# A hybrid decoder layer: mixer work placed as single hops between dense products, TensorE in program order

## The chip, the cores and the metric

The kernel runs on one core of a Trainium2 chip. Five engines work side by side, each through its own instruction queue: TensorE (matmuls, PE in the profile, its weight loads PEld), VectorE (DVE), ScalarE (ACT), GpSimd (POOL) and SyncE (SP), whose queue issues the DMA transfers here. The metric is the device time of one execution in microseconds, the median of several runs: 2523.2 us before (three runs, 2522.54 to 2525.14).

## The reference

One decoder layer over x of 2048 tokens by 1024 channels, all float32, conditioned by a vector c:

```python
mod = silu(c) @ w_ada + b_ada                       # six rows of 1024
shift1, scale1, gate1, shift2, scale2, gate2 = split(mod, 6)
h = rmsnorm(x, norm1_w) * (1 + scale1) + shift1
proj = h @ w_in          # 2312 columns: q 512, k 128, v 128, z 512, x/B/C 1024, dt 8
attn = sliding_window_attention(rope(q), rope(k), v, sinks)   # 8 query, 2 key heads, window 128
xbc = silu(causal_depthwise_conv(xbc, conv_w, conv_b))        # width 4
y = ssd_chunked_scan(xs, softplus(dt + dt_bias), -exp(a_log), B, C, d_skip)   # 8 heads, state 128, chunks of 128
y = groupnorm(y * silu(z)) * ssm_norm_w
x = x + gate1 * (concat(attn, y) @ w_out)
h = rmsnorm(x, norm2_w) * (1 + scale2) + shift2
x = x + gate2 * ((silu(h @ w_gate) * (h @ w_up)) @ w_down)    # 2816 hidden
return rmsnorm(x, final_norm_w)
```

The scan carries a state from chunk to chunk, so the SSD chunks depend on each other in order; attention looks at the chunk and the one before it.

## The kernel before

Tokens are cut into four blocks of 512 (b = 0 to 3), each of four tiles of 128. Every dense product is computed as three products: each float32 operand is split into a rounded part `hi` and the rest `lo` (`split`, `halves`, `weight`), and `mm3` (L216-219) accumulates hi x hi, hi x lo and lo x hi. `weight` (L203) loads 256 KB of a weight into `raw`, rounds it on ACT (L212) and subtracts on POOL (L213); each block does so again for all weights of the input and the output projection.

The **mixer phase** goes over the blocks. `in_proj(b, h)` yields after each dense piece: queries, keys and values (`tokens`, 256 or 264 columns a matmul), eight groups of convolution channels (L355, 24 matmuls of 512 columns each) and the gate z. Results go to DRAM. Beside it run the **mixers**, which are Python generators: `attentions(b)` (scores, softmax, values, on PSUM banks `at` and `am`) and `ssds(b)` (banks `st` and `sm`). A hop is a group of matmuls whose result an ACT or DVE instruction has to read before the next group can start. `beside` (L919) advances the mixers by `RATIO` = 1.6 steps per dense piece; one step holds several hops. `finish(ssd_of[b - 1])` (L953) runs what is left of a block's scan in blocks 1 and 2, before `out_proj(b - 1)`; the output projection of blocks 0 and 1 lies in this phase, that of blocks 2 and 3 in the down-projection. `ada` computes a row of `mod`: a 512 KB load and a product with the sum over the row, 16 rows ahead of the first block (eight of them shared between POOL and ACT), 32 later through the one buffer `aw`.

The **up-projection** (`quads`, `operands`, seven products in place of eight per 2 x 2 group, L753-755) runs for blocks 0 and 1, with the attention of block 3 and the scan of blocks 2 (its rest) and 3 beside it at `RATIO_UP` = 0.55 steps per product; then down-projections of blocks 0 and 1, the up-projection of blocks 2 and 3, and their down-projections.

What sets the order: the program is traced in Python order, and a planner then places the instructions of every engine, TensorE too, by a cost model and by when their inputs are due, so the order on an engine isn't that of the text. `issue_after` adds an edge on one engine. Within an engine the queue is strictly in order on the chip. Tile pools have a fixed number of buffers per tag (`w` 6, `raw` 5, `hl` 8, `it` 3, four PSUM banks `d`); a new tile waits until an old one's last reader is done.

Of the kernel before, what the change touches and what calls it, by code (L numbers as in the profile page):

```python
# [17 lines left out]
P = 128  # L18
# [13 lines left out]
RATIO, RATIO_UP = 1.6, 0.55  # L32
# [10 lines left out]
def hymba_layer(ctx, tc, xT, crow, pos, wada, vecs, rows, wq, wkv, wz, wx, wo, wgu, wd4, wd2, outT):  # L43
# [5 lines left out]
    sb = mixing.enter_context(tc.tile_pool(name="mix", bufs=1, side="right"))  # L49
    ip = projecting.enter_context(tc.tile_pool(name="inp", bufs=1))  # L50
# [22 lines left out]
    def m2(dt=F32):  # L73
        return big("m2", M2, dt)

    def m4():
        return sb.tile([P, 2, T], F32R, name="m4", tag="m4", bufs=M4)

    def m1():
        return small([P, 2 * P], "m1", M1)  # L80
# [30 lines left out]
    later_f = big("it", 3, pool=ip)[:, 0:P]  # L111
# [21 lines left out]
    for i in range(2):  # L133
        cs, th = csil[:, i * T:(i + 1) * T], big("it", 3, pool=ip)
        nc.scalar.activation(th, cs, AF.Tanh, scale=0.5)
        nc.vector.scalar_tensor_tensor(cs, th, 1.0, cs, ALU.add, ALU.mult)
    mod = const([P, 48], "mod", pool=cst)

    def ada(i, tag, bufs, shared=False):
        w = ip.tile([P, 2, T], F32, name=tag, tag=tag, bufs=bufs).rearrange("p h t -> p (h t)")  # L140
        load = nc.sync.dma_start(w, wada[i])
        m = mod[:, i:i + 1]
        if shared:
            nc.gpsimd.tensor_tensor(w, w, csil, ALU.mult)
            nc.scalar.activation(w, w, AF.Copy, scale=0.5, accum_out=m)
            nc.vector.tensor_tensor(m, m, b_ada[:, i:i + 1], ALU.add)
        else:
            nc.vector.tensor_tensor_reduce(w, w, csil, 0.5, b_ada[:, i:i + 1], ALU.mult, ALU.add, m)
        return load
# [10 lines left out]
    def rope_tables():  # L160
        posf = const([P, S // P], "posf", pool=ip)
        nc.vector.tensor_copy(posf, posi)
        ang = big("it", 3, pool=ip)
# [3 lines left out]
        for dst, turn in ((sin, 0.0), (cos, 0.25)):  # L167
            k, r = big("it", 3, pool=ip), big("it", 3, pool=ip)
# [34 lines left out]
    def weight(src, n=T, own=None):  # L203
        if own is None:
            raw = wt.tile([P, 528], F32, name="raw", tag="raw", bufs=RAW)
            two = wt.tile([P, 2, 528], F32R, name="w", tag="w", bufs=SPLIT)
        else:
            raw = own.tile([P, T], F32, name="rawo", tag="rawo", bufs=2)
            two = own.tile([P, 2, T], F32R, name="wo", tag="wo", bufs=2)
        hi, lo = two[:, 0, :n], two[:, 1, :n]  # L210
        nc.sync.dma_start(raw[:, :n], src)
        nc.scalar.activation(hi, raw[:, :n], AF.Copy)  # L212
        nc.gpsimd.tensor_tensor(lo, raw[:, :n], hi.bitcast(F32), ALU.subtract)  # L213
        return hi, lo
# [33 lines left out]
    def modulated(x, bc, scale, shift):  # L248
        h = tmp()
        nc.vector.scalar_tensor_tensor(h, x, scale, bc, ALU.mult, ALU.mult)  # L250
        hi, lo = pair("hl", 8, pool=ip)
# [8 lines left out]

    def norm1(b, h):
        acc = tmp()
        for d in range(KT):
            square_into(acc, load_x(b, d), d == 0)
        y = rstd(acc)
        yield
        bc = spread(y)
        for d in range(KT):
            h.append(modulated(load_x(b, d), bc, scl1[:, d:d + 1], sh1[:, d:d + 1]))
# [9 lines left out]
    def in_proj(b, h):  # L279
        dt_of[b] = small([P, NT, 8], "dt", 3)  # L280

        def tokens(srcs, n, toks):
            per = 2 if n == 256 else 1
            banks = [dense() for _ in range(len(toks) // per)]
            plan = [(i, t, banks[i // per][:, i % per * n:i % per * n + n]) for i, t in enumerate(toks)]
            for kp in range(KT // 2):
                whi, wlo = weight(srcs[kp], 2 * n)
                for e in range(2):
                    k, cs = 2 * kp + e, slice(e * n, (e + 1) * n)
                    for i, t, out in plan:  # L290
                        ts = slice(t * P, (t + 1) * P)
                        mm3(out, h[k][0][:, ts], h[k][1][:, ts], whi[:, cs], wlo[:, cs],
                            k == 0 and i % per == 0, k == KT - 1 and i % per == per - 1)
            return [(t, out) for _, t, out in plan]

        def tokens_by_k():
            qb = [dense() for _ in range(NT)]
            for kp in range(KT // 2):
                ws = [weight(wq[c][kp], 512) for c in range(2)]
# [8 lines left out]
            return qb  # L308

        def rope(dst, src, heads, gt):  # L310
            s4 = src.rearrange("p (h two j) -> p h two j", two=2, j=HALF)
            d4 = dst.rearrange("p (h two j) -> p h two j", two=2, j=HALF)
            tm = big("it", 3, pool=ip)[:, :heads * 64]
            t4 = tm.rearrange("p (h two j) -> p h two j", two=2, j=HALF)
            c = cos[:, gt, :].unsqueeze(1).broadcast_to([P, heads, HALF])
            s = sin[:, gt, :].unsqueeze(1).broadcast_to([P, heads, HALF])
            for i in range(2):
                nc.vector.tensor_tensor(d4[:, :, i, :], s4[:, :, i, :], c, ALU.mult)
                nc.vector.tensor_tensor(t4[:, :, i, :], s4[:, :, 1 - i, :], s, ALU.mult)
            for i, op in ((0, ALU.subtract), (1, ALU.add)):  # L320
                nc.gpsimd.tensor_tensor(d4[:, :, i, :], d4[:, :, i, :], t4[:, :, i, :], op)

        every = range(NT)

        def put_q(part, got):
            for t, ps in got:
                q = small([P, 256], "sq", 2, pool=ip)
# [3 lines left out]
        def put_kv(got):  # L331
            for t, ps in got:
                kv = small([P, 2 * P], "skv", 2, pool=ip)
# [3 lines left out]
                nc.sync.dma_start(kv_d[b * NT + t], kv)  # L337

        def keys_values():
            for half in range(2):  # L340
                put_kv(tokens(wkv, 264, (2 * half, 2 * half + 1)))
                yield

        if b == 0:
            for t, ps in enumerate(tokens_by_k()):
                q = m2()
                rope(q, ps, 8, t)
                nc.sync.dma_start(q_d[t], q)
            yield
        else:  # L350
            for part in range(2):
                put_q(part, tokens(wq[part], 256, every))
                yield
        yield from keys_values()
        for c in range(8):  # L355
            ps = dense()
            for half in range(2):
                whi, wlo = weight(wx[c, half])
# [8 lines left out]
            cv, th, o = big("it", 3, pool=ip), big("it", 3, pool=ip), big("sx", 2, pool=ip)  # L367
# [6 lines left out]
            in_proj.last = nc.vector.scalar_tensor_tensor(o, th, 1.0, cv, ALU.add, ALU.mult)  # L374
            nc.sync.dma_start(xs_d[b][c], o)
            yield
        for part in range(2):
# [673 lines left out]
```

## Time and profile before

| | |
|---|---|
| median of three runs | 2523.2 us (2522.54 to 2525.14) |
| profiled execution | 2513.37 us, span 2511.7 us |
| TensorE busy | 2288.0 us, 91% |
| VectorE busy | 1478.8 us, 59% |
| ScalarE busy | 1063.3 us, 42% |
| GpSimd busy | 1490.7 us, 59% |
| DMA | 336.51 MB, mean 134 GB/s |
| mean granted TensorE clock | 0.951 |

All numbers of a profile come from one execution, the profiled one, whose own time is some 10 us below the median of the others. A busy share is a mean over stages; matmuls overlap, so a busy TensorE isn't one at its peak. In a row of groups stand line, engine, operation, tiles written and read, shapes and count, then busy time, mean ns of one instruction, and the idle time just before them with what ended it. A row of waits has the waiting engine, tile and line, the releaser, the total, how often and the longest.

### The profile page before, as it was taken

The page shows a single profiled execution, that of the slowest core. Times are in us where ns is not written, and L with a number is a line of the kernel's source. Part 1 is how long each engine was busy: PE and PEld are TensorE (multiplying, and loading weights), DVE is VectorE, ACT ScalarE, POOL GpSimd, SP SyncE. Part 2 cuts the span into 40 slices and gives each one's busy share as a digit, 9 for nine tenths or more (in the row PEclk, how much of TensorE's full clock was granted, in tenths as well). Part 3 has the DMA queues.
Part 4 walks back from the last instruction along what each step waited for, and adds up shares of the span by engine and source line. Part 5 has one row for each costly group of instructions (what it writes and reads, how often), then busy time and mean ns, then how long its engine had stood idle before and what let it go on. Part 6 is the DMA issues. An engine that isn't in the chain of part 4 may idle for free.

```text
span 2511.7 us, 33257 instructions
## 1 busy us (share of the span) xinstructions
PE 2288.0 (91%) x11198; PEld 1899.1 (76%) x11198; DVE 1478.8 (59%) x2451; ACT 1063.3 (42%) x2172; POOL 1490.7 (59%) x1412
## 2 busy tenths in 40 slices
PE   3778896999699969999999999998999999999896
PEld 2667784798478857888888788876788888878685
DVE  8587655456644597565775544369555555454544
ACT  3454553556354634445343334334333333333332
POOL 6754764477535778555886545547666666643442
PEclk9899896999789979999999999999999999999998
DMA  6567552444344432221323455464332222253341
GB/s 237 190 197 237 170 176 70 152 159 156 120 139 127 137 111 88 82 82 64 117 89 118 155 171 193 144 216 164 98 133 76 76 80 85 88 214 101 127 166 51
DMA packets 208810, 336.51 MB, mean 134 GB/s; under 512 B 20608, under 2 KB 66688, under 8 KB 208640
## 3 DMA queue, kind: packets, MB, share of 16 engines
q1 hardware_dynamic: 207488, 333.35, 40.1%
q8 instruction: 88, 1.44, 0.2%
q10 hardware_dynamic: 1152, 1.05, 0.1%
q14 instruction: 82, 0.67, 0.1%
HBM read 267.21 MB, written 67.11 MB: 133 GB/s over the span
## 4 chain that ended last, share of the span: by engine, by line
PE 62%; DVE 5%; POOL 2%; issue 1%; DMA 1%; ACT 1%; SPq 0%; DVEq 0%; POOLq 0%; ACTq 0%
PE d L755 8%; PE d L753 8%; PE d L754 8%; PE d L217 7%; PE d L218 7%; PE d L219 7%; PE am L217 1%; PE am L219 1%; PE am L218 1%; PE st L753 1%; PE st L755 1%; PE am L755 1%; PE am L754 1%; PE st L754 1%; PE am L753 1%
## 5 line engine op out<-in xcount | busy, mean ns | idle before, releaser
L699 ACT ACTIVATE w<-raw 128x512 fp32r<-128x512 f32 x308 | 193.4, 630 | 453.5 <-PE d L219 230.2
L753 PE MATMUL d<-b,w 128*128 128x512 f32 x924 | 368.8, 400 | 8.2 <-ACT b L732 7.2
L755 PE MATMUL d<-b,w 128*128 128x512 f32 x924 | 368.1, 399 | 3.0 <-DVE w L700 3.0
L754 PE MATMUL d<-b,w 128*128 128x512 f32 x924 | 368.4, 399 | 0.8 <-DVE b L727 0.8
L217 PE MATMUL d<-a,w 128*128 128x512 f32 (+1 forms) x720 | 281.7, 398 | 18.3 <-DVE x L832 9.9
L700 POOL TENSOR_TENSOR w<-s,w 128x512 fp32r<-128x512 f32 x132 | 190.2, 1441 | 161.9 <-ACT w L699 160.2
L213 POOL TENSOR_TENSOR w<-raw,w 128x512 fp32r<-128x512 f32 (+1 forms) x160 | 218.6, 1375 | 113.2 <-ACT w L212 97.5
L218 PE MATMUL d<-a,w 128*128 128x512 f32 (+1 forms) x720 | 282.6, 393 | 2.2 <-DVE a L694 2.2
L219 PE MATMUL d<-a,w 128*128 128x512 f32 (+1 forms) x720 | 281.7, 391 | 0.0
L700 POOL TENSOR_TENSOR w<-raw,w 128x512 fp32r<-128x512 f32 x88 | 124.8, 1419 | 200.8 <-ACT w L699 194.4
L832 DVE SCALAR_TENSOR_TENSOR x<-d,mod,x 128x512 f32<-128x512 f32 (+1 forms) x182 | 131.2, 724 | 167.3 <-PE d L219 163.7
L700 DVE TENSOR_TENSOR w<-raw,w 128x512 fp32r<-128x512 f32 x220 | 188.7, 858 | 48.5 <-ACT w L699 42.8
L217 PE MATMUL d<-w,hl 128*128 128x256 f32 (+1 forms) x640 | 189.1, 298 | 27.2 <-ACT hl L252 17.5
L753 PEld LDWEIGHTS d<-b,w 128*128 128x128 f32 x924 | 175.3, 190 | 48.3 <-ACT b L732 8.3
L755 PEld LDWEIGHTS d<-b,w 128*128 128x128 f32 x924 | 175.0, 189 | 41.8 <-DVE w L700 3.4
L754 PEld LDWEIGHTS d<-b,w 128*128 128x128 f32 x924 | 175.5, 190 | 41.0 <-DVE b L727 1.1
L218 PE MATMUL d<-w,hl 128*128 128x256 f32 (+1 forms) x640 | 188.9, 297 | 0.9 <-POOL w L213 0.9
L219 PE MATMUL d<-w,hl 128*128 128x256 f32 (+1 forms) x640 | 183.0, 297 | 1.8 <-DVE hl L253 1.8
L217 PEld LDWEIGHTS d<-a,w 128*128 128x128 f32 x720 | 136.8, 190 | 53.3 <-ACT a L821 11.6
L699 ACT ACTIVATE w<-s 128x512 fp32r<-128x512 f32 x176 | 110.1, 628 | 128.6 <-PE d L755 80.6
L218 PEld LDWEIGHTS d<-a,w 128*128 128x128 f32 x720 | 137.2, 191 | 33.7 <-DVE a L694 4.1
L219 PEld LDWEIGHTS d<-a,w 128*128 128x128 f32 x720 | 137.2, 191 | 31.6 <-issue 0.2
(313 smaller groups left out, 5708.2 us busy)
## 6 DMA issues: line engine op xcount, KB each, us to landing
raw<-in_wgu_dram SPq DMA_DIRECT2D x176, 256.0 KB, 2.7
raw<-in_wd_dram SPq DMA_DIRECT2D x176, 256.0 KB, 2.6
act<-t SPq DMA_DIRECT2D x88, 256.0 KB, 2.1
t<-act SPq DMA_DIRECT2D x88, 256.0 KB, 4.3
t<-in_xT_dram SPq DMA_DIRECT2D x80, 256.0 KB, 3.7
rawo<-in_wo_dram SPq DMA_DIRECT2D x64, 256.0 KB, 2.8
raw<-in_wx_dram SPq DMA_DIRECT2D x64, 256.0 KB, 2.9
aw<-in_wada_dram SPq DMA_DIRECT2D x32, 512.0 KB, 3.7
```

The lines of the kernel that those rows point to most:

```text
L213: nc.gpsimd.tensor_tensor(lo, raw[:, :n], hi.bitcast(F32), ALU.subtract)
L217: nc.tensor.matmul(out, ahi, bhi, start=first, stop=False)
L218: nc.tensor.matmul(out, ahi, blo, start=False, stop=False)
L219: mm3.last = nc.tensor.matmul(out, alo, bhi, start=False, stop=last)
L699: nc.scalar.activation(hi, x, AF.Copy)
L700: eng.tensor_tensor(lo, x, hi.bitcast(F32), ALU.subtract)
L753: nc.tensor.matmul(out, ahi, bhi, start=first and k == 0, stop=False, skip_group_check=True)
L754: nc.tensor.matmul(out, ahi, blo, start=False, stop=False, skip_group_check=True)
L755: mm3.last = nc.tensor.matmul(out, alo, bhi, start=False, stop=k == 3, skip_group_check=True)
L832: nc.vector.scalar_tensor_tensor(x, ps, gate2[:, c:c + 1], x, ALU.mult, ALU.add)
```

## The change

- In the mixer phase TensorE's instructions are issued in program order (`tc.manual_schedule` for that engine); the other engines are still planned.
- Dense pieces are cut finer: half a convolution group, a quarter of a 256-column product, half an output group. `attentions` and `ssds` are rewritten so that one step is one hop on TensorE; `both` alternates between the two. `tick` counts dense pieces, advances the mixers (`MIX` = 1.2 per piece, 0.5 in block 0 and at the end) and calls `pending` work (the norms' small matmuls) some pieces later.
- Blocks 0 and 1 get attention and scan beside the projections; a second pool `extra` gives the scan its own buffers. Attention 2 runs beside the output projection of block 1 and the convolution of block 3. The scans of blocks 2 and 3 and attention 3 stand beside the first up-projection, at `RATIO_UP` = 0.6.
- `weight` stores the split pair of a projection weight to DRAM when it is first made (x, z and out in block 0, q and the second half of k/v in block 1); later blocks load the pair, 512 KB, with no work on ACT or POOL. Block 0's q and k/v and the first half of block 1's k/v are split without a store.
- `ada` is on DVE alone; the 32 later rows come as two loads of 256 KB each into one buffer of half the size. The ring `hl` grows from 8 to 12 and also holds the output projection's operands; tag `it` goes over to the ring `s`. The out-projection's own weight ring `wo` is dropped for the shared `w`. The operands of the up-projection get their tiles in order of use.

```diff
-RATIO, RATIO_UP = 1.6, 0.55
+MIX, RATIO_UP = 1.2, 0.6
...
+    common, extra = tiles(sb, M1, M2, M4), tiles(xp, 4, 10, 4)
...
-    def ada(i, tag, bufs, shared=False):
...
+    def ada_halves(i):
+        for half in range(2):
+            w, hs = big("aw", 1, pool=ip), slice(half * T, (half + 1) * T)
+            nc.sync.dma_start(w, wada[i, :, hs])
+            nc.vector.tensor_tensor_reduce(w, w, csil[:, hs], 0.5, (part if half else b_ada)[:, i:i + 1],
+                                           ALU.mult, ALU.add, (mod if half else part)[:, i:i + 1])
...
-    def weight(src, n=T, own=None):
...
+    def weight(src, n, key, store):
+        two = wt.tile([P, 2, 528], F32R, name="w", tag="w", bufs=SPLIT)
         hi, lo = two[:, 0, :n], two[:, 1, :n]
+        if key in split_d:
+            nc.sync.dma_start(two[:, :, :n].bitcast(F32), split_d[key])
+            return hi, lo
+        raw = wt.tile([P, 528], F32, name="raw", tag="raw", bufs=RAW)
         nc.sync.dma_start(raw[:, :n], src)
         nc.scalar.activation(hi, raw[:, :n], AF.Copy)
         nc.gpsimd.tensor_tensor(lo, raw[:, :n], hi.bitcast(F32), ALU.subtract)
+        if store:
+            split_d[key] = dr.tile([P, 2, n], F32, name="w_" + "_".join(str(k) for k in key))
+            nc.sync.dma_start(split_d[key], two[:, :, :n].bitcast(F32))
         return hi, lo
...
+    def operand():
+        return pair("hl", 12, pool=ip)
...
+            whi, wlo = weight(srcs[kp], 2 * n, (name, kp), b == (0 if name[0] == "z" else 1) and toks[-1] == NT - 1)
...
+            if kp < KT // 2 - 1 and (per == 2 or kp % 2):
+                yield
...
+                if half:
+                    yield
+                whi, wlo = weight(wx[c, half], T, ("x", c, half), b == 0)
...
             for j in range(4):
                 if held:
-                    held.pop(0)()
-                sms.append(scores(st, qhi, qlo, slots, j))
-                if j % 2:
-                    yield
+                    held[0](j)
+                sms.append(scores(m, st, qhi, qlo, slots, j))
+                if j == 3:
+                    probabilities(st, sms, slots)
+                yield
+                if held and j % 2:
+                    held[1](j // 2)
+                    if j == 1:
+                        yield
...
+    def tick(ratio):
+        for entry in list(pending):
+            entry[0] -= 1
+            if entry[0] == 0:
+                pending.remove(entry)
+                entry[1]()
+        due[0] += ratio
+        while due[0] >= 1.0:
+            due[0] -= 1.0
+            while sides and next(sides[0], sides) is sides:
+                sides.pop(0)
...
+    def both(*gens):
+        live = list(gens)
+        while live:
+            for g in list(live):
+                if next(g, g) is g:
+                    live.remove(g)
+                else:
+                    yield
...
+    def norm_ahead(b):
+        h = []
+        g = norm1(b, h)
+        next(g)
+        pending.extend([[8, lambda: next(g)], [12, lambda: next(g)]])
+        return h
...
+    with tc.manual_schedule(engines={mybir.EngineType.PE}):
+        run(queries(0, h), 0)
+        run(keys_values(0, h), 0)
+        prepared(0)
+        att = attentions(0, common)
+        sides.append(att)
...
+        run(with_ada(convolved(0, h)), 0.5)
+        run(with_ada(gated(0, h)), 0.5)
+        sides[:] = [both(att, ssds(0, stepping[0], extra))]
+        mix0 = sides[0]
+        h = nxt
+        run(with_ada(queries(1, h)), MIX)
+        run(with_ada(keys_values(1, h)), MIX)
+        prepared(1)
+        nxt = norm_ahead(2)
+        run(with_ada(convolved(1, h)), MIX)
+        run(gated(1, h), MIX)
+        drain(rest)
+        mix1 = both(attentions(1, common), ssds(1, stepping[1], extra))
+        sides.append(mix1)
+        h = nxt
+        run(queries(2, h), MIX)
+        run(keys_values(2, h), MIX)
+        prepared(2)
+        run(convolved(2, h), MIX)
+        finish(mix0)
+        out = out_proj(0, y_of, lambda c: operand(), lambda c: dense())
+        nxt = norm_ahead(3)
+        run(gated(2, h), MIX)
+        next(out)
+        next(out)
+        run(out, MIX)
+        h = nxt
+        run(queries(3, h), MIX)
+        run(keys_values(3, h), MIX)
+        finish(mix1)
+        prepared(3)
+        sides.append(spaced(attentions(2, common), 1))
+        out = out_proj(1, y_of, lambda c: operand() if c % 2 else halved(extra.m4()), lambda c: dense())
+        next(out)
+        next(out)
+        run(out, 0.5)
+        run(convolved(3, h), 0.5)
+        run(gated(3, h), 0.5)
+        finish(sides[0] if sides else None)
+    for b in (2, 3):
+        if b == 3:
+            sides.append(attentions(3, common))
+        sides.append(ssds(b, stepping[b], common))
```

More of the change, by code (lines that the diff above doesn't have):

```diff
@@ L277, in hymba_layer, with staged @@
     dt_of = {}
[L279 to L296, printed above, removed]
+    def staged():
+        return small([P, 256], "so", 4, pool=ip)
@@ L337, in put_kv, with convolved @@
                 nc.sync.dma_start(kv_d[b * NT + t], kv)
[L339 to L354 removed]
+            yield
+    def convolved(b, h):
         for c in range(8):
@@ L611, in ssd @@
-        st = bank("sm", 1)
-        for g in range(2):
-            nc.tensor.matmul(st[:, g * 256:(g + 1) * 256], btok[:, g * P:(g + 1) * P], xdte[:, g * 256:(g + 1) * 256],
-                             start=True, stop=True)
-        new = big("state", 2)
-        if old is not None:
-            nc.gpsimd.tensor_tensor(by_head(new), by_head(old), bc64(etot), ALU.mult)
-            nc.vector.tensor_tensor(new, new, st, ALU.add)
-        else:
-            nc.vector.tensor_copy(new, st)
-        carry["state"] = new
@@ L661, in out_proj @@
+        yield
+        turned(*out)
+        yield
+    def out_proj(b, y_of, into, bank_of, norm=None):
         mix = []
```

455 lines of the change are left out of this document (241 added, 214 removed).

## Prediction

> **What bounds the kernel now.** I read the page first for where TensorE is not full, then cut the span into stages at the places where the dense products stop, and asked each stage for its waits. Times are us.
>
> ```profile
> span 2511.7 us, 33257 instructions
> PE 2288.0 (91%) x11198; PEld 1899.1 (76%) x11198; DVE 1478.8 (59%) x2451; ACT 1063.3 (42%) x2172; POOL 1490.7 (59%) x1412
> ...
> PE   3778896999699969999999999998999999999896
> ...
> PEclk9899896999789979999999999999999999999998
> DMA  6567552444344432221323455464332222253341
> ```
>
> Slices are 62.8 us. From the sixteenth slice on TensorE is nearly full at full clock; the holes lie in the first fifteen, the mixer phase. The busy time of each stage (columns: length, then busy time and instructions of PE, PEld, DVE, ACT, POOL, the granted clock, DMA share, GB/s):
>
> ```profile
> 0.00:132.00 132.00, 71.70 (x399) 63.45 (x400) 94.77 (x155) 52.07 (x92) 91.35 (x118) 0.94 0.61 209
> 132.00:445.00 313.00, 253.11 (x1448) 218.45 (x1447) 203.96 (x423) 156.61 (x363) 171.85 (x209) 0.85 0.54 172
> 360.00:445.00 85.00, 57.28 (x220) 41.14 (x220) 50.97 (x92) 29.58 (x75) 34.15 (x70) 0.64 0.35 110
> 445.00:706.00 261.00, 232.11 (x1338) 198.79 (x1337) 144.83 (x336) 141.76 (x335) 156.70 (x194) 0.89 0.45 144
> 628.00:706.00 78.00, 53.59 (x223) 39.39 (x222) 46.61 (x91) 31.78 (x81) 35.26 (x69) 0.69 0.39 120
> 706.00:960.00 254.00, 226.50 (x1307) 194.92 (x1307) 156.94 (x315) 133.97 (x309) 169.19 (x176) 0.93 0.39 124
> 884.00:960.00 76.00, 54.48 (x225) 41.41 (x225) 70.15 (x92) 34.21 (x76) 59.44 (x63) 0.78 0.30 94
> 960.00:1300.00 340.00, 339.81 (x1673) 282.92 (x1672) 219.59 (x347) 154.39 (x353) 227.43 (x213) 1.00 0.27 90
> ```
>
> I call **lost** what TensorE idles plus what it runs below full clock: (length - busy) + busy x (1 - clock). That gives 97.9 for 132-445 (59.89 + 253.11 x 0.15), 54.4 for 445-706, 43.4 for 706-960 and 0.2 for 960-1300; the rest, 215.1, 206.6 and 210.6, is work. Most of the loss sits in three short stretches: 48.3 of 85 in 360-445, 41.0 of 78 in 628-706, 33.5 of 76 in 884-960. The waits of the first of them (line, what it waited for, total, times, longest):
>
> ```profile
> PE st L636 <- ACT m L633: 6.4, 3, 4.5
> PE at L468 <- DMA m<-q: 2.9, 1, 2.9
> PE st L604 <- ACT m L639: 2.5, 2, 1.2
> PE sm L597 <- DVE m L592: 2.4, 3, 1.1
> ```
>
> They are all links of one SSD chain: a hop on TensorE, its reader on ACT or DVE, the next hop. `finish` runs the rest of `ssds` there with nothing dense beside it, and the clock falls too:
>
> ```profile
> 391.19 0.39 PE L217 MATMUL d<-mo,wo 128*128 128x512 f32 x1
> 391.42 0.39 PE L218 MATMUL d<-mo,wo 128*128 128x512 f32 x1
> ...
> 415.21 0.63 PE L588 MATMUL sm<-m,later_r 128*128 128x512 f32 x1
> ```
>
> A matmul of 512 columns takes 0.39 among dense work and 0.63 in the chain; dense ones start 0.23 apart. The Trainium skill ("TensorE: Matmul & The Clock Gate", What's actually happening) has the clock halve after an idle window of about 3.4 us. Here no single wait but one reaches that and the clock still stood at 0.64; by the page's rule the new hops, if each waits a us or two, would keep full clock, by the row they would not.
>
> **The change, part by part.**
>
> Single hops between dense pieces. A dense piece is now 24 matmuls of 256 columns or 12 of 512, about 2.8 us at the 0.23 spacing, and 1.2 hops follow each. By the yields, an attention is 32 hops and an SSD 26. Block 0 gives 12 hops (24 pieces at 0.5), block 1 has 36 pieces and 43 hops, the next 28 + 25 pieces give 63: attention and SSD of blocks 0 and 1 (116 hops) end inside dense work, so the stretches at 360 and 628 vanish as such. Blocks' two mixers alternate, so between two hops of one chain lie 1.7 pieces and one foreign hop, near 5.6 us, against chain waits of 1 to 4.5 in the rows. That covers most hops; 136 are so placed. Attention 2 runs at 0.5 beside 41 pieces: 20 hops, and its last 12 are run bare by `finish`. At the old bare price (48.3 lost for about 26 hops, 1.9 each) these cost 23.
>
> TensorE in program order removes the planner's freedom to fill a late hop with later dense work. What is queued behind a late hop is everything on TensorE. This price isn't in the trace; bounds: below nothing excluded only where the stretch is already full (445-628 ran at 178.52 busy of 183), above by the bare 1.9 per hop. I take it near the covered end, inside the shares below.
>
> Split weights in DRAM. The rows that price a split, and the transfers:
>
> ```profile
> L213 POOL TENSOR_TENSOR w<-raw,w 128x512 fp32r<-128x512 f32 (+1 forms) x160 | 218.6, 1375 | 113.2 <-ACT w L212 97.5 <-issue 15.0 <-POOL w L213 0.3
> L212 ACT ACTIVATE w<-raw 128x512 fp32r<-128x512 f32 (+1 forms) x160 | 99.0, 630 | 64.6 <-PE d L219 47.6 <-DMA raw<-in_wx_dram 7.4 <-POOL w L213 5.4
> ...
> raw<-in_wx_dram SPq DMA_DIRECT2D x64, 256.0 KB, 2.9
> ```
>
> Loads of ready pairs: x 48, z 24, q 16, k/v 16, out 48, together 152. POOL is relieved of 152 x 1.375 = 209, ACT of 152 x 0.63 = 96. Neither engine is full in any stage above, so on TensorE's path this is worth nothing by itself; it shortens queues. Against it stand bytes: each pair load is 0.52 MB instead of 0.26, and 52 pairs are stored. The first full stage, 132-445, moved 172 GB/s x 313 = 53.8 MB in 0.54 x 313 = 169 of all engines' time, 3.14 per MB. Into it now fall 24 pairs stored in block 0, 12 in block 1 (36 x 0.52 = 18.9 MB) and 24 pair loads (6.3 MB more than raw): 79 MB, **248 of DMA time**, more than TensorE's 215 and DVE's 204. This is the step that I take to limit the gain. How dense DMA can get, in slices of 7.8 of that stage:
>
> ```profile
> DMA  8655656684966687683634343357586414021115
> GB/s 283 203 201 156 214 148 222 216 287 159 307 220 226 216 257 242 190 297 124 192 113 145 123 134 103 103 162 228 158 258 239 150 53 133 34 67 53 34 50 168
> ```
>
> One slice reaches 0.9, five reach 0.8. I take 0.90, because stores can wait and six `w` buffers look some 17 us ahead: 248 / 0.90 = 276. The Trainium skill ("DMA: Bandwidth & Descriptors", the table at its head) puts a core's share of HBM at about 358 GB/s; by that 79 MB take an estimated 221, TensorE and DVE would set the stage, and the sum would be that of the rival in which transfers don't bind.
>
> The conditioning. `ada_halves` doubles the loads of `aw` to 64 of half the size with one buffer. It shares a queue with every DVE consumer:
>
> ```profile
> L148 DVE CUSTOM_DVE_ANT_0 aw<-aw,csil,vec 128x1024 f32<-128x1024 f32 x26 | 41.4, 1594 | 30.5 <-DMA aw<-in_wada_dram 30.5
> ```
>
> DVE work stays 41.4; its blocked time may go from 30.5 to twice that, 61. In 276 DVE then has 204 + 61 = 265 used, so it is just covered; without that cover the two would add. The first norm's eight products move from POOL and ACT to DVE, eight times about 1.3, in a stage of 132 with DVE at 94.77; the squares' sums move too. POOL no longer runs beside them. I cost the start at nothing, with 10 either way.
>
> SSD of block 2 moves into the up-projection: 82 hops over 154 products at 0.6 (92 places) where 37 coarser steps stood. Its TensorE work only changes place. In 960-1300 side work was hidden fully (339.81 of 340), so I charge 4, bounds 0 and 20 as POOL has 227 there already. The operands for that stage take tiles in order of use, so the first can start in the space that `extra` leaves. I keep their wait:
>
> ```profile
> PE d L753 <- ACT b L732: 7.2, 2, 4.9
> ```
>
> Doubled for the half clock that follows, 14.
>
> **The sum.** 132-445: 313 to 276, 37 won (bounds: -27 with DMA at 0.73, 60 with TensorE 85% full). 445-706: extra bytes are 40 pair loads and 16 stores, 18.9 MB, so DMA goes from 117 to 177 and doesn't bind; 206.6 of work at 0.92 full, between 132-445 (215 of 313) and the best, 445-628, is 225: 36 won (10 to 48). 706-960: 43.4 lost becomes 23 + 14 + 3: 3 won (-25 to 25). Later: 4 given back. Together 72. The profiled execution took 2513.4 (span 2511.7), so 2441; the median of the runs shown, 2523.2, is 9.8 above the profiled one. **2451.**
>
> **Rivals.** *Transfers don't bind* (for: 0.8 and more for whole slices; against: 52 stores that hold their `w` buffer until they land). Then 132-445 takes 215 / 0.85 = 253 (60 won), 445-706 takes 206.6 / 0.97 = 213 (48 won), the end wins 15: 119 with the 4 given back, 2404. *Transfers bind harder*: no slice of 62.8 is above 0.73 (the fourth, `7` on the page, 188 to 251, where the share row of the finer view shows only short peaks). 248 / 0.73 = 340 for the first stage, 27 lost; 36 + 3 - 4 remain: 2515. *In-order stalls*, the one that ends slower: a late reader on DVE holds the hop, the hop holds all dense work, no other piece may pass. Lost time in 132-960 was 195.7; with 37 for the bare end, 136 hops may lose 159 before nothing is won, 1.17 each. At 1.5, between that and the bare 1.9, 204 + 37 are lost: 45 more and the 4, 2572. For it: DVE near full in block 1. Against: 5.6 us of cover. *It does what it says but only moves holes* (the bare 12 hops, one `d` bank and the `hl` ring held by the next norm at each block's end): four block ends at 10 each take 40 of the 72, 2491.
>
> **Chances.** Forecast 0.47 (own range 2425 to 2475); transfers free 0.22; holes move 0.08; transfers bind harder 0.10; in-order stalls 0.13. Range 2365 to 2520: it takes in the first, third and fourth case to their bounds and leaves out most of the stalls and a tail of the second. A change of 0.2% (5 us) is about what this kernel's runs tell from none. Faster: 0.47 + 0.22 + 0.08 and half of the fourth case, less a little for its lower bounds, 0.80; the same 0.06; slower 0.14.
>
> **What would show it.** Right: the page's digits of PE without the two holes at slices 7 and 11; no SSD chain at half clock between dense stretches; DMA share about 0.85 or more from block 0's convolution to the end of block 1, `w` loads landing later than 2.9; POOL's split group at 72 instances instead of 224. A hole of about 35 is left just before the up-projection, waits of `at` and `am` on ACT and DVE. Wrong: TensorE waiting on DVE or ACT readers all over blocks 1 and 2 (the stall case), or no stage with DMA near full and TensorE above 0.9 there (transfers free).

## The result, and the profile after

| | median us (lowest to highest) | ratio to before, 95% interval |
|---|---|---|
| before, beside the changed kernel | 2523.98 | 1 |
| changed kernel, four runs | 2463.78 (2462.67 to 2467.43) | 0.976 [0.975, 0.978] |

The change makes the kernel 60 us faster, 2.4%. The forecast was 2451, 13 us lower. The profiled execution of the changed kernel took 2463.4, its span is 2461.7, and its mean granted clock is 0.963 instead of 0.951.

The page of the changed kernel, busy times and slices (61.5 us each):

```profile
span 2461.7 us, 32964 instructions
PE 2246.5 (91%) x11198; PEld 1877.8 (76%) x11198; DVE 1439.6 (58%) x2526; ACT 967.5 (39%) x2004; POOL 1255.0 (51%) x1249
...
PE   1969789899899699999999998899799999999996
...
PEclk9979999999899799999999999899899999999998
DMA  5778867867876233222334654664322222263451
...
L225 POOL TENSOR_TENSOR w<-raw,w 128x512 fp32r<-128x512 f32 (+1 forms) x72 | 98.3, 1373 | 129.6 <-ACT w L224 109.1
...
w<-w_x SPq DMA_DIRECT2D x48, 512.0 KB, 5.3
w<-w_o SPq DMA_DIRECT2D x48, 512.0 KB, 4.5
```

The two holes of the kernel before, in its seventh and eleventh slices, are gone. Two shallower ones are there instead, in the third slice and the fifth. The one just before the up-projection, in the fifteenth slice before, is still there, in the fourteenth. POOL and ACT are relieved of the splits, and DMA stands at 6 to 8 tenths from the second slice to the thirteenth.

I divide both executions at the first product of each dense stage:

| start of the stage, us | before | after | before minus after |
|---|---|---|---|
| first dense matmul | 45.0 | 50.5 | -5.5 |
| up-projection 1 | 905 | 814 | 91 |
| down-projections 0, 1 | 1434 | 1363 | 71 |
| up-projection 2 | 1789 | 1728 | 61 |
| its last product | 2225 | 2179 | 46 |
| end of the span | 2511.7 | 2461.7 | 50 |

So the mixer phase won 91 and 41 of it were given back later: 20 in the first up-projection, 10 in the down-projections, 15 in the second up-projection, with 4 regained at the end. The stages by windows (length, then busy time and instructions of PE, PEld, DVE, ACT, POOL, granted clock, DMA share, GB/s), first before: mixer phase, first up-projection, down-projections, second up-projection.

```profile
92.00:905.00 813.00, 702.71 (x4112) 609.14 (x4111) 473.75 (x1059) 420.66 (x978) 485.69 (x575) 0.90 0.49 156
905.00:1434.00 529.00, 512.70 (x2399) 420.07 (x2398) 340.57 (x493) 231.67 (x505) 355.96 (x331) 0.97 0.28 93
1434.00:1789.00 355.00, 343.74 (x1471) 276.65 (x1470) 212.30 (x293) 140.84 (x237) 200.13 (x142) 0.99 0.52 176
1789.00:2225.00 436.00, 432.28 (x1858) 349.26 (x1857) 230.23 (x265) 143.97 (x244) 279.72 (x199) 1.00 0.27 90
```

The same stages after, and then four stretches of it:

```profile
92.00:814.00 722.00, 635.19 (x3902) 565.76 (x3900) 423.94 (x1080) 332.96 (x809) 295.77 (x420) 0.93 0.77 254
814.00:1363.00 549.00, 530.50 (x2550) 439.01 (x2550) 362.03 (x526) 247.69 (x552) 383.92 (x361) 0.97 0.31 96
1363.00:1728.00 365.00, 346.89 (x1470) 276.48 (x1470) 185.12 (x272) 115.30 (x191) 138.52 (x101) 0.98 0.59 192
1728.00:2179.00 451.00, 438.55 (x1858) 352.63 (x1858) 261.71 (x288) 153.86 (x260) 293.32 (x207) 0.98 0.28 90
...
20.00:40.00 20.00, 0.00 (x0) 0.00 (x0) 20.00 (x34) 4.31 (x7) 9.07 (x6) 1.00 0.99 381
100.00:160.00 60.00, 40.51 (x168) 32.83 (x169) 31.07 (x86) 30.09 (x70) 37.17 (x38) 0.80 0.82 290
180.00:220.00 40.00, 37.55 (x304) 37.23 (x303) 25.14 (x52) 22.86 (x59) 18.73 (x16) 0.96 1.00 350
...
800.00:860.00 60.00, 37.48 (x161) 28.25 (x160) 55.42 (x80) 33.60 (x76) 37.44 (x26) 0.72 0.29 90
```

By the prediction's measure of lost time the mixer phase went from 180.6 (110.29 + 702.71 x 0.10) to 131.3 (86.81 + 635.19 x 0.07). Of what is left, 27.6 sits in 100-160. The stretch 800-860 loses 33.0, but only 5.7 of it ahead of the first product of the up-projection at 814; the rest belongs to that stage, whose operands are still being prepared. The kernel before lost 33.5 at the same place (its 884-960), so this hole hasn't changed. DVE is busy for 55.42 of its 60 us, as it was for 70.15 of 76 before, which points to the preparation on DVE; no run tests it. TensorE's waits of the changed kernel from 50 to 860:

```profile
PE d L247 <- POOL t L242: 32.3, 2, 19.3
PE d L232 <- ACT m L210: 9.4, 1, 9.4
PE d L794 <- ACT b L769: 7.6, 3, 3.0
PE st L607 <- ACT m L687: 6.5, 2, 4.7
PE am L232 <- DVE k_ring L487: 6.4, 2, 4.8
PE at L564 <- DVE m L568: 5.8, 4, 2.3
PE am L232 <- DVE ast L541: 5.6, 5, 3.1
```

The largest isn't a mixer hop. It is the norm of the next block, whose sum over channels is done by eight small matmuls (`rstd`, L247) that stand in TensorE's program order, some pieces after the norm was started. They come to the head of the queue before POOL has added up the squares (`t`, L242). TensorE's timeline, start and length of the group and the idle time before it:

```profile
139.22 1.87 PE L247 MATMUL d<-ones,t 128*128 128x2 f32 x8 [19.25 <-POOL t L242]
```

The eight x loads of this sum are issued one by one among the other transfers, the first at 94.4, the last at 130.0, and the last lands at 135.3. POOL adds the last four squares between 133.43 and 139.17. Why the planned order spreads these loads so far no run shows. SP's timeline, which issues the transfers, shows what stands behind them: four half rows of `ada_halves`, of which the last three wait in SP's queue (5.7, 3.8 and 3.2 us), since there is only one buffer `aw`. The four take 14.08 us in all, and the x load behind them is the first of the norm's second pass over x, so they don't make this sum late.

```profile
128.95 1.46 SPq L273 DMA_DIRECT2D t<-in_xT_dram  x3
130.45 14.08 SPq L158 DMA_DIRECT2D aw<-in_wada_dram  x4
144.63 0.38 SPq L273 DMA_DIRECT2D t<-in_xT_dram  x1
```

### The profile page after: what moved, and what is told of

Read it like the earlier page. It is cut to its first block, busy times and chain, and to the rows that moved or that the text cites. A ratio compares the mean times of both kernels' runs of the same rounds, so it can differ in the third digit from the quotient of the medians.

```text
span 2461.7 us, 32964 instructions
## 1 busy us (share of the span) xinstructions
PE 2246.5 (91%) x11198; PEld 1877.8 (76%) x11198; DVE 1439.6 (58%) x2526; ACT 967.5 (39%) x2004; POOL 1255.0 (51%) x1249
## 4 chain that ended last, share of the span: by engine, by line
PE 73%; DVE 7%; DMA 6%; ACT 2%; issue 1%; POOL 1%; SPq 0%; DVEq 0%; POOLq 0%; ACTq 0%
PE d L233 10%; PE d L234 10%; PE d L232 10%; PE d L794 9%; PE d L796 8%; PE d L795 8%; DMA aw<-in_wada_dram 4%; PE am L232 1%; PE am L233 1%; PE am L234 1%; DVE aw L159 1%; DVE b L770 1%; PE sm L673 1%; PE st L794 1%; PE st L796 1%
## 5 line engine op out<-in xcount | busy, mean ns | idle before, releaser
L743 POOL TENSOR_TENSOR w<-raw,w 128x512 fp32r<-128x512 f32 x88 | 118.7, 1349 | 296.2 <-ACT w L742 277.7
L743 DVE TENSOR_TENSOR w<-raw,w 128x512 fp32r<-128x512 f32 x220 | 194.6, 885 | 69.6 <-ACT w L742 66.9
L232 PE MATMUL d<-w,hl 128*128 128x256 f32 (+1 forms) x640 | 186.9, 292 | 2.0 <-ACT hl L267 1.6
L234 PE MATMUL d<-w,hl 128*128 128x256 f32 (+1 forms) x640 | 183.7, 287 | 3.7 <-DVE hl L268 3.7
L233 PE MATMUL d<-w,hl 128*128 128x256 f32 (+1 forms) x640 | 184.1, 288 | 0.0
L242 POOL TENSOR_TENSOR t<-t 128x512 f32<-128x512 f32 (+1 forms) x84 | 106.8, 1272 | 128.6 <-ACT t L241 121.7
L225 POOL TENSOR_TENSOR w<-raw,w 128x512 fp32r<-128x512 f32 (+1 forms) x72 | 98.3, 1373 | 129.6 <-ACT w L224 109.1
```

Source lines behind the costliest of these rows:

```text
L232: nc.tensor.matmul(out, ahi, bhi, start=first, stop=False)
L233: nc.tensor.matmul(out, ahi, blo, start=False, stop=False)
L234: mm3.last = nc.tensor.matmul(out, alo, bhi, start=False, stop=last)
L242: eng.tensor_tensor(acc, acc, sq, ALU.add)
L743: eng.tensor_tensor(lo, x, hi.bitcast(F32), ALU.subtract)
```

## The experiments

Each kernel was timed in several rounds beside the kernel before; ratios are to that, with their 95% interval. All but `e4_before_pairs` start from the changed kernel. The kernel before read 2522.74 beside the first four of these runs (`e1` to `e4`), 2521.89 beside the next four and 2521.14 beside the last three, against 2523.98 beside the changed kernel; so the difference of two runs from different rounds is uncertain by up to 3 us, and for small ones I also give it with each run set against the kernel before of its own rounds.

### TensorE planned again (`e1_planned`)

```diff
-    with tc.manual_schedule(engines={mybir.EngineType.PE}):
+    if True:
```

> The changed kernel with one part undone: TensorE's order in the mixer phase is left to the planner again; single hops, stored pairs and everything else stay. If program order itself carries the gain, the time goes back to 2490 or more. If the finer hops carry it and program order only costs, since a late matmul at the head of the queue then holds up all others (as the norm's sums did for 19 and 13 us), it falls to about 2440. If the order makes no difference, 2460 within 6.

Measured: 2430.45, 0.963 [0.962, 0.965], 33 us faster than the changed kernel. Program order costs time. The windows of its mixer phase and of 60 us with DMA nearly full, and then TensorE's waits from 50 to 860:

```profile
88.00:773.00 685.00, 637.63 (x3923) 567.32 (x3921) 422.70 (x1081) 333.90 (x809) 301.86 (x423) 0.95 0.80 268
...
180.00:240.00 60.00, 59.90 (x498) 59.41 (x497) 44.71 (x114) 25.48 (x61) 44.13 (x58) 1.00 0.97 336
```

```profile
PE am L232 <- DVE ast L541: 12.8, 11, 3.4
...
PE at L564 <- DVE m L568: 6.0, 5, 1.9
...
PE d L247 <- POOL t L242: 3.7, 2, 2.9
```

The norm's wait falls from 32.3 to 3.7, and that for the output projection's operand on ACT (L210) from 9.4 to 1.4: the planner lets other dense matmuls go ahead of them. The waits of single hops are not shorter (`ast` 12.8 in eleven waits instead of 5.6 in five). This run also bears on the transfers: the same instructions move the same weights in a phase that is 37 us shorter, at 0.80 instead of 0.77, and TensorE is busy for 59.90 of 60 at full clock while DMA stands at 0.97.

### The pairs split again in each block (`e2_resplit`), and the pairs alone (`e4_before_pairs`)

```diff
-        if store:
+        if False:
```

> The changed kernel without the stored pairs: every projection weight is loaded raw and split again in each block, 67 MB less to move, 152 splits more on ACT (0.63 us each) and POOL (1.37 us each). If transfers bound the mixer phase, as the prediction had it, DMA's share there falls from about 0.8 to 0.6 and the time falls to about 2440. If the splits were what held TensorE, it rises to 2480 or more. If neither binds, 2464 within 6.

Measured: 2510.23, 0.995 [0.993, 0.997]. Without the stored pairs the change is worth 12.5 us (against 2522.74) instead of 60. The second kernel puts nothing but the pairs into the kernel before:

```diff
+        if key in split_d:
+            nc.sync.dma_start(two[:, :, :n].bitcast(F32), split_d[key])
+            return hi, lo
...
+        if store:
+            split_d[key] = dr.tile([P, 2, n], F32, name="w_" + "_".join(str(k) for k in key))
+            nc.sync.dma_start(split_d[key], two[:, :, :n].bitcast(F32))
```

> The kernel before with the stored pairs alone: coarse mixer steps and the planner's order as before. If transfers are what the pairs load up, it is slower than before, 2525 to 2540; if the freed ACT and POOL time shortens the mixers' chains, it is faster, 2500 to 2515; if neither matters at this order, 2524 within 6.

Measured: 2476.88, 0.981 [0.979, 0.983]: 46 us from the pairs alone (46 to 48 when they are taken from the changed kernel), and 12.5 from all the rest. The two parts add up to the whole, 58 against 60. Mixer phase of `e2_resplit`, and then ACT's largest waits in it:

```profile
92.00:857.00 765.00, 646.37 (x3896) 571.33 (x3894) 468.74 (x1079) 398.85 (x928) 451.18 (x540) 0.92 0.53 162
```

```profile
ACT w L224 <- PE d L234: 124.8, 65, 8.4
ACT m L552 <- DVE ast L548: 36.8, 11, 7.5
```

Its DMA share is lower by a third and it takes 43 longer. ACT stands 125 us at the head of its queue with a split whose `w` buffer TensorE still reads, and behind it wait the softmax and the scan, whose results TensorE needs. The same wait in the kernel before, for the two rings of weights, and in the changed kernel, where it is left for the weights that are still split:

```profile
ACT w L212 <- PE d L219: 40.9, 37, 4.3
ACT wo L212 <- PE d L219: 26.2, 15, 4.3
```

```profile
ACT w L224 <- PE d L234: 26.7, 12, 10.6
```

On TensorE two waits for the mixers' readers have grown, from 5.8 and 6.4 in the changed kernel to these in `e2_resplit`:

```profile
PE at L564 <- DVE m L568: 19.1, 7, 7.7
PE am L232 <- DVE k_ring L487: 17.8, 6, 7.9
```

I read this as the cost of a split that "neither engine is full" leaves out. DVE shows a second one, below: 468.74 for 1079 instructions against 423.94 for 1080.

### What of the splits costs the time (`e5_busy_kept`, `e10_busy_paced`)

Both keep the pair loads and add to each, in the phase of the projections, one copy on ACT and one subtraction on POOL whose results nobody reads. In the first they read a constant:

```diff
+            if projecting_open[0]:
+                idle = wt.tile([P, 528], F32, name="raw", tag="raw", bufs=RAW)[:, 0:T]
+                nc.scalar.activation(idle, csil[:, 0:T], AF.Copy)
+                nc.gpsimd.tensor_tensor(idle, idle, csil[:, T:2 * T], ALU.subtract)
```

> The changed kernel with the stored pairs, but for each of the 120 pair loads of the mixer phase ACT and POOL still do one copy and one subtraction of 128x512, on a scratch tile that depends on no transfer and on no w buffer (ACT 120 x 0.63 = 76 us, POOL 120 x 1.3 = 156 us). If the stored pairs help because ACT and POOL have less to do, most of the 46 us come back: 2495 or more. If they help because no split stands at the head of ACT's queue any more, waiting for TensorE to free a w buffer (119 us of ACT in the run that splits again), it stays at 2464 to 2474.

Measured: 2578.31, 1.022 [1.020, 1.024]. It does not answer its question. As nothing held the extra work back, the planner piled it up. A window of it and TensorE's longest wait:

```profile
300.00:360.00 60.00, 4.42 (x15) 3.60 (x16) 20.40 (x29) 26.20 (x47) 58.33 (x50) 0.51 0.24 74
```

```profile
PE st L612 <- ACT m L692: 91.0, 3, 83.5
```

One reader behind that pile held one hop of the scan, and in program order all of TensorE, for 83.5. In the second kernel the extra work reads the pair that has just landed, so it keeps the pace of the loads:

```diff
+                idle = wt.tile([P, 528], F32, name="raw", tag="raw", bufs=RAW)
+                nc.scalar.activation(idle[:, :n], hi.bitcast(F32), AF.Copy)
+                nc.gpsimd.tensor_tensor(idle[:, :n], idle[:, :n], hi.bitcast(F32), ALU.subtract)
```

> As the run with the work of ACT and POOL kept, but the copy and the subtraction read the pair that has just landed, so that they come one pair at a time and not in one burst; they still wait for no w buffer to be freed by TensorE. If less work on ACT and POOL is what the stored pairs bring, most of the 46 us come back: 2495 or more. If it is the wait for a w buffer at the head of ACT's queue, 2464 to 2475.

Measured: 2502.48, 0.993 [0.990, 0.996]: 39 of the pairs' 46 us are lost again (42 with each set against the kernel before of its own rounds), though the `w` buffers are filled by DMA alone as in the changed kernel. Its mixer phase:

```profile
92.00:864.00 772.00, 645.99 (x3936) 573.78 (x3935) 484.51 (x1100) 406.31 (x942) 473.69 (x550) 0.92 0.73 239
```

TensorE waits for a `w` load for only 0.6 us in all here. So the gain is for the most part not that a weight reaches TensorE sooner, but what no longer stands in the queues of ACT and POOL, and through POOL also on DVE, in front of the mixers' readers. One thing stays open: the extra copies also wait at ACT's head for the load to land, some 146 us over 76 waits (`w_kv` 44.3, `w_x` 30.4, `w_q` 27.9, `w_o` 24.6, `w_z` 18.3), so work and waiting in ACT's queue are not told apart.

### The norm's small matmuls later (`e3_norm_later`)

```diff
-        pending.extend([[8, lambda: next(g)], [12, lambda: next(g)]])
+        pending.extend([[at[0], lambda: next(g)], [at[1], lambda: next(g)]])
```

with `at` = (14, 18) for the norms of blocks 1 and 2.

> The changed kernel with the norm's small matmuls for blocks 1 and 2 called at pieces 14 and 18 in place of 8 and 12. If the holes of 19 us at 120 and 13 us at 300 come from these matmuls standing in program order ahead of their sums of squares, both close and the time falls by 20 to 32, to 2432 to 2444. If transfers set the pace, the same bytes still have to come and the holes only move: 2460 within 6.

Measured: 2466.64, 0.977 [0.975, 0.979], no change. One of the two waits is gone: the sums of block 2 come at 325 without one, and TensorE's waits for the norm fall from 32.3 to 17.8. But others have come, the largest of them absent from the changed kernel, and the wait of block 1 is still there, 16 us later:

```profile
155.09 1.87 PE L247 MATMUL d<-ones,t 128*128 128x2 f32 x8 [17.81 <-POOL t L242]
```

```profile
PE d L232 <- DVE so L401: 15.1, 3, 5.5
```

The edit moves the small matmuls alone; x loads and squares are called where they were. But their engines are planned, and in the trace the last of block 1's eight x loads is issued at 147.9 instead of 130.0: they moved along. A later place in the text did not give this matmul more lead, and the lead that block 2's got was worth nothing in time.

### Two buffers for the half rows (`e6_aw_two`)

```diff
-    common, extra = tiles(sb, M1, M2, M4), tiles(xp, 4, 10, 4)
+    common, extra = tiles(sb, M1, M2, M4), tiles(xp, 4, 9, 4)
...
-            w, hs = big("aw", 1, pool=ip), slice(half * T, (half + 1) * T)
+            w, hs = big("aw", 2, pool=ip), slice(half * T, (half + 1) * T)
```

> The changed kernel with two aw buffers in place of one (and one m2 buffer of the second pool less, to make the space). If SP standing at the head of its queue on the one aw buffer (14 us in one piece from 130 on) is what keeps the norm's x and the weights late around 120 to 140, that hole shrinks and the time falls by 10 to 20, to 2445 to 2455. If the loads that matter are ahead of it in the queue, 2464 within 6.

Measured: 2456.90, 0.974 [0.972, 0.975], 7 us faster (5 with each set against the kernel before of its own rounds). DVE's waits from 50 to 860, after and in this kernel:

```profile
DVE aw L159 <- DMA aw<-in_wada_dram: 85.4, 41, 7.6
```

```profile
DVE aw L159 <- DMA aw<-in_wada_dram: 36.1, 24, 8.1
```

The blocked time falls by 49, but the two waits of the norm on POOL stay, 40.6 together with one of 21.1. That agrees with SP's timeline: the half rows stand behind the loads of the sum.

### Attention 2 earlier (`e7_att2_early`)

```diff
-        run(out, 0.5)
-        run(convolved(3, h), 0.5)
-        run(gated(3, h), 0.5)
+        run(out, 0.8)
+        run(convolved(3, h), 0.8)
+        run(gated(3, h), 0.8)
```

> The changed kernel with attention 2 advanced by 0.8 in place of 0.5 hops per piece beside the output projection of block 1 and block 3's convolution and gate, so that none of its hops is left to be run bare. If the bare hops cost what the prediction charged (23 us), 2440 to 2450. If the operands of the up-projection set the end of the phase anyway, 2460 within 6.

Measured: 2478.15, 0.983 [0.981, 0.985]: 14 us slower, which neither branch of the expectation allows. With 0.8 all 32 hops find a dense piece, and the up-projection begins at 831 instead of 814. The last hops of attention 2 had not been bare: in the changed kernel the last of them run until after 868, beside the preparation of the up-projection's operands, in which TensorE has little to do anyway. Without them the hole stays: from 831 to 880 of this run TensorE is busy for 21.94 of 49 us at a clock of 0.55, and DVE for 47.03. I did not follow where in block 3 the denser hops cost their time.

### The second up-projection (`e8_ops_as_before`, `e9_out_whole`)

The 15 us lost there could come from the order in which operands get their tiles, or from the finer output projections of blocks 2 and 3 that run just before. The first gives the operands of blocks 2 and 3 their tiles one k after the other, as in the kernel before:

```diff
-            ops.setdefault(n, []).extend(pair("b", 28, pool=bp) for _ in range(count))
+            ops.setdefault(n, []).extend(pair("b", 28, pool=bp) for _ in range(count if first else 0))
...
+                if not first:
+                    ops[name].append(pair("b", 28, pool=bp))
```

> The changed kernel with the operand tiles of the second up-projection allocated k by k as before (the first one's stay in order of use). The second up-projection took 451 us in place of 436. If the order of tiles makes its operands late, about 2450; if the later place of the norm or the output projection does it, 2464 within 6.

Measured: 2464.06, 0.975 [0.972, 0.979], nothing (one of its four runs took 2451.64, the others 2463.43 and more). The second lets these two output projections yield a whole group again; those of blocks 0 and 1 stay fine:

```diff
-                if half:
+                if half and norm is None:
                     yield
```

> The changed kernel with the output projection of blocks 2 and 3 (the ones beside the down-projection) yielding once per output group as before, in place of twice; blocks 0 and 1 keep the halves. If the finer yields are what makes these two end 44 us before the second up-projection instead of 128, so that its operands are late (451 us in place of 436, and 365 in place of 355 before it), about 2440 to 2450. If something else delays them, 2464 within 6.

Measured: 2449.11, 0.972 [0.970, 0.974], 15 us faster (12 with each set against the kernel before of its own rounds), and the stage is back at its old length:

```profile
1726.00:2161.00 435.00, 431.28 (x1855) 349.41 (x1855) 230.96 (x265) 144.03 (x243) 278.41 (x197) 0.99 0.27 90
```

The output projections of blocks 2 and 3 are advanced by a fixed ratio per product of the down-projection. With two steps where one was, at the same ratio, they ended later: their last matmul starts 64 us before the second up-projection, instead of 127 in the kernel before and 123 here. (The expectation's 128 is this distance before, but its 44 is that of the last matmul of the norm behind the projections, which is 104 before and here.) What hangs on them, norm and operands of blocks 2 and 3, then ran into the up-projection. TensorE's waits from 1680 to 1800 in the changed kernel show it; in `e9_out_whole` the first is not there and the second is 1.9:

```profile
PE d L794 <- ACT b L774: 4.8, 3, 2.4
PE d L232 <- DVE x L873: 3.2, 4, 1.3
```

The down-projections ahead of it still take 366 us, against 365 in the changed kernel and 355 before: these 10 are not explained.

### Together (`e11_combined`)

The edits of `e1_planned`, `e6_aw_two` and `e9_out_whole` in one kernel.

> TensorE's order left to the planner, two aw buffers (one m2 of the second pool less), whole output groups in blocks 2 and 3; single hops and stored pairs stay. If the three act in different places their gains add: 2464 - 33 - 7 - 18 = 2406, between 2395 and 2420. If they mend the same lateness, 2425 to 2435.

Measured: 2411.16, 0.957 [0.955, 0.959]: 53 us faster than the changed kernel and 110 faster than the one before in its own rounds. The three gains, 33 + 7 + 15 = 55, add up almost in full (with each run set against the kernel before of its own rounds, 32 + 5 + 12 = 49, and 50 together). Its mixer phase, with the up-projection at 767:

```profile
86.00:767.00 681.00, 638.57 (x3938) 566.92 (x3936) 431.65 (x1084) 335.64 (x813) 305.21 (x426) 0.95 0.80 271
```

Its lost time by the measure is 74.4, against 131.3 in the changed kernel and 180.6 before.

## Why the prediction was right, and where it was wrong

The direction was right and the time lay within the forecast's own range (2425 to 2475). But of the 72 us of the sum hardly one term came from where it was placed; two errors took each other back, and that the number fell inside the range is in good part luck.

- **The holes at 360 and 628 vanish.** Right: no SSD chain stands between dense stretches, and of `st`, the scan's bank, TensorE's leading waits from 50 to 860 hold only 6.5.
- **Split weights: "on TensorE's path this is worth nothing by itself".** Wrong, and the largest error. The pairs alone bring 46 us; they were the larger part of the gain. The step failed where it took ACT at 42% and POOL at 59% as free. My reading is that a queue costs by what stands at its head: a split that waits for its `w` buffer (67 us on ACT in the kernel before, 125 in `e2_resplit`) stands in front of the reader of a hop. `e10_busy_paced` doesn't tell this wait from the work itself. The size of the relief was right: POOL's group has 72 instances, as forecast.
- **"This is the step that I take to limit the gain": 248 us of DMA in the first stage.** Wrong as a limit, right as a load. The share of 0.87 and 0.83 in 100-200 and 200-300 is what was named, and `w` loads, with twice the bytes, land in 4.5 to 5.3 instead of 2.9. But the cap of 0.90 doesn't exist here: 180-220 ran at 1.00, and `e1_planned` moved the same pairs 37 us faster with TensorE at 59.90 of 60 beside a share of 0.97. The Trainium skill ("DMA: Bandwidth & Descriptors", the table at its head) gives about 358 GB/s as a core's share of HBM, and further down it calls that the share with two cores streaming. The 381 GB/s in 20-40 agree with the second statement, so that table alone doesn't make 221 us, the prediction's estimate from it, a floor; whether the first stage could move its bytes faster no run shows. Of the rivals, *transfers don't bind* had the mechanism, and its 2404 failed on the next step.
- **Program order, "taken near the covered end".** Wrong by 33 us, as `e1_planned` shows. *In-order stalls* was right that it costs, but not about which instruction: 136 hops were in the sum, and the two waits that grew most are the norm's sums (32.3 against 3.7) and the output projection's operand (9.4), which the step didn't count among what stands in line. `e5_busy_kept` shows the rule at its worst, 83.5 for one late reader. The price per hop, 1.17 to break even, would be 0.24 if all 33 were put on the 136.
- **The bare end.** The size came out, 23 + 14 = 37 forecast and 33.0 lost in 800-860, by luck. The kernel before had lost 33.5 there. Hops and operands overlap, so their prices don't add, and giving the hops cover made it 14 slower and left the hole (`e7_att2_early`). What both executions share is a DVE that is busy for over nine tenths of the stretch.
- **Later stages, "I charge 4".** Right for the moved scan, wrong for what it left out. The first up-projection is 20 longer with 151 more matmuls, and its lost time by the measure went from 31.7 to 34.4, 3 more, about what the rounding of the clock allows: moved work, and so paid for by the mixer phase. But 25 went in the down-projections and the second up-projection. The 15 of the latter are the finer yields at an unchanged ratio (`e9_out_whole`); the 10 of the former stay open. The prediction followed the finer pieces in the mixer phase and not in the other place where `out_proj` is run.
- **The start, at nothing with 10 either way.** 5.5 lost. DVE was busy for 20.00 of 20 in 20-40, with TensorE idle.
- **The conditioning, "may go from 30.5 to twice that".** DVE was blocked for 85.4, more than that. The second buffer, which takes 49 of this away, is worth 5 to 7 (`e6_aw_two`). The one buffer also held SP's queue, as in the stretch of 14.08, which the step didn't name.

In sum: the mixer phase won 91, with the start's 5.5 in it, where 76 were forecast, since 46 came unforeseen from the pairs and no transfer is seen to take its toll, while order took back 33. Behind it 41 were given back, 20 of them moved work, where 4 were forecast. What the single hops bring without the rest, the finer pieces and the second pool of buffers above all, no run separates.

## What to carry to other kernels

An engine that is half idle can still cost time: 46 us of this gain came from work taken off engines at 42% and 59%. Price work that is removed by what waits behind it, not by the engine's share. If one engine is put in program order, list everything in its stream that reads a late result, norms and operands too and not only the chains that the order was written for; the planned order was 33 us faster here with the same pieces. When a generator is cut finer, each place that advances it by a ratio changes its speed.

## What the runs showed of the hardware

**DVE runs slower beside POOL.** The convolution's L392 on DVE and the scan's L601 have one shape each and durations from 0.68 to 1.9 us. The source view of both lines (shortest, median and longest ns, first and last start), after and then in `e2_resplit`:

```profile
L392 DVE SCALAR_TENSOR_TENSOR sx<-s x32: 677/692/1768, 108.6 to 782.6; 128x512 f32<-128x512 f32 x32
L601 DVE TENSOR_TENSOR m<-m,m x16: 680/692/1775, 227.6 to 556.5; 128x512 f32<-128x512 f32 x16
```

```profile
L392 DVE SCALAR_TENSOR_TENSOR sx<-s x32: 677/948/1894, 111.3 to 830.2; 128x512 f32<-128x512 f32 x32
L601 DVE TENSOR_TENSOR m<-m,m x16: 677/1162/1793, 246.0 to 597.5; 128x512 f32<-128x512 f32 x16
```

The shortest are equal; the medians go from 692 to 948 and 1162 when POOL is busy for 451 us instead of 296. Taken one by one in the two traces, the 33 of these instructions during which POOL does nothing take 677 to 695 ns, and during each one above 800 POOL is busy for at least 0.44 of its time. The Trainium skill ("SBUF — State Buffer", Who interferes with whom) states that a DVE instruction with two inputs in SBUF contends with a GpSimd instruction that reads SBUF; these rows agree. I hadn't counted on it as part of what the splits cost: 45 us of DVE time in the mixer phase.

**The clock falls without a long wait.** In 800-860 it was granted at 0.72, and no wait of TensorE in that window is longer than 3.1. The prediction weighed the Trainium skill ("TensorE: Matmul & The Clock Gate", What's actually happening), which names an idle window of about 3.4 us as what halves the clock, against the row of 0.64 in the kernel before. This window sides with the row: the clock fell though no single wait was that long.
